# The opening of a decoder trunk: where the first shift vector is summed, and how the first matmul units follow

## The chip, the cores and the metric

The kernel runs on one core of one Trainium2 chip. Its time is the device time of one launch in microseconds (us). Three runs of the kernel before took 1204.4, 1201.04 and 1201.66 us, a median of 1201.66 us. The engines are named as in the profile: PE (matmuls; PEld its weight loads), DVE (vector), ACT (scalar), POOL (GpSimd) and SP, which here only issues transfers.

## The reference

Two layers act on a sequence of 256 rows of width 1024. Each layer is a SwiGLU feed-forward part (FFN), a token-mixing part and a second FFN, and each of the three reads a normalised and modulated input. Only the very first one matters here:

```python
c_act = jax.nn.silu(c)
mod = c_act @ w_ada[l] + b_ada[l]                      # 9 vectors of 1024
sh1, sc1, gt1, sh2, sc2, gt2, sh3, sc3, gt3 = jnp.split(mod, 9, axis=-1)
h = rmsnorm(x, ln_ffn1_g[l]) * (1 + sc1) + sh1         # modulate
x = x + 0.5 * gt1 * (silu(h @ w_gate) * (h @ w_up)) @ w_down
```

Each of the nine vectors is the product of one row of 1024 values with a 1024 x 1024 matrix: 4 MB of weights for one vector. The first FFN needs the scale vector `sc1` and the shift vector `sh1` before anything else.

## The kernel before, in words

Everything is held transposed, channels on partitions: `xT` is 8 blocks of 128 channels x 256 rows. A weight is brought in by granules of 1 MB (`raw`, four buffers, issued by SP) and cut into units of 128 output columns x 1024. The numbers are f32; a unit is split into a high part `hi` (a cast on ACT to the matmul format) and a low part `lo` (a subtraction, on DVE, for a few early units on POOL). There are six unit buffers. A product is three matmuls for each block: hi x hi, hi x lo, lo x hi, so a unit is 24 matmuls of 128x256.

A modulation vector is four granules of `w_ada`. DVE sums them: for each of eight blocks one instruction `acc = raw * c + acc` on 128x1024 (tiles `Lb` and `adaacc`, function `ada_step`). `extract` then sums over partitions with eight PE transposes and two reductions, and `complete` adds the bias.

The list `seq` sets the order in which granules are loaded and used (`plan_ffn`, `adaunit`). Before, it begins with the scale vector (0, 1), then the first gate granule, the first up granule, the second gate granule, then the four granules of the shift vector (0, 0), then the second up granule. SP issues a granule only when its buffer is released.

The first FFN starts without the shift (`first`, the branch where `G["sh"]` is None). Since the norm factor is one number for each row, `(x*gs) @ W` can be computed before the norm is known, and the shift's part `sh @ W` is added as a bias for each column. Six units (gate 0 and 1, up 0 and 1, gate 2 and 3) run one behind the other (`low_last`), then PE waits for the shift vector. With it, 96 narrow matmuls make `sh @ W` for the six units (tile `sh_b`, two stationary columns), and `turn_row` turns these rows into biases. Up 2 and 3, and everything behind, use the finished modulated input `H`.

Later phases do it in another way (the other branch of `first`): the input has two more columns that hold the split shift, so that a matmul of 258 columns gives `sh @ W` along with the rest, and the bias is copied from column 256 (`cols`). Four units start that way, and the fifth already uses `H`.

`columns(0, 1)` turns rows of small constants into columns: two PE transposes into the same PSUM tile `px`, each followed by a DVE copy (`colA`, `colB`). The second transpose may not start before the first copy has read `px`. `keep_warm` is a few matmuls whose result nobody reads.

The order on each engine is that of the program text; `pump` and `step_stream` put conversions and sums into it by modelled times. `down 0` below is the first unit of the first FFN's down projection, `pa<-Y,hi` in the profile: from there on PE does the same work in both kernels.

Of the kernel before, what the change touches and what calls it, by code (L numbers as in the profile page):

```python
# [177 lines left out]
def trunk(ctx, tc, t, out):  # L178
# [121 lines left out]
    def plan_ffn(l, which, ada):  # L300
        wg, wu, wd = (t[f"ffn{which}_w_{n}"][l] for n in ("gate", "up", "down"))
        jobs = []
        gd = {}
        key = ("f", l, which)

        def down(f):
            if f % 2 == 0:
                gd[f // 2] = rgran(wd, 128 * f)
            wunit(key + ("d", f), gd[f // 2], rview(f % 2))

        slots = FB - 2 if len(ada) > 4 else FB // 2
        start = 4 if key == ("f", 0, 1) else 0
        at = {}
        for i, item in enumerate(ada):
            at.setdefault(start + i * (slots - start) // len(ada), []).append(item)

        def extra(slot):
            for item in at.pop(slot, ()):
                adaunit(*item)

        for q in range(FB // 2):
            for n, w in (("g", wg), ("u", wu)):
                g = kgran(w, 256 * q, 256)
                for j in range(2):
                    wunit(key + (n, 2 * q + j), g, kview(256, j))
                if key == ("f", 0, 1) and (q, n) == (1, "g"):
                    for i in range(4):
                        adaunit(0, 0, i)
            if q:
                extra(2 * q - 2)  # L330
                for j in range(2):
                    down(2 * q - 2 + j)
                extra(2 * q - 1)
        down(FB - 2)
        down(FB - 1)
        assert not at
# [72 lines left out]
    for i in range(4):  # L409
        adaunit(0, 1, i)  # L410
# [68 lines left out]

    def ada_step(item):  # L480
        _, (l, v), g, i, _ = item
        raw = grans[g]["tile"].rearrange("p (k n) -> p k n", n=D)
        if i == 0:
            tag = "adaacc" if (l, v) in ADA["m", 0] + ADA["m", 1] or cfg["tag"] == "Lb" else "Lb"
            cfg["tag"] = tag
            while any(job[1].tensor.name.startswith(tag) for job in ada_wait):
                extract()
            ada_acc[l, v] = sb([128, D], tag)
        acc = ada_acc[l, v]
        for j in range(2):  # L490
            k = 2 * i + j
            c = c_act[:, k:k + 1]
            if k == 0:
                dve.tensor_scalar(acc, raw[:, j], c, 0.0, op0=OP.mult, op1=OP.add)
            else:
                dve.scalar_tensor_tensor(acc, raw[:, j], c, acc, op0=OP.mult, op1=OP.add)
        release(g)
        if i == 3:
            ada_wait.append([(l, v), acc, 0])
# [169 lines left out]
    def begin(gs, sh):  # L669
# [4 lines left out]
        if sh is not None:  # L674
            hi, lo = split_col(sh)
            for src, piece, k, n in ((hi, 0, 0, 6), (hi, 1, 6, 2), (lo, 2, 0, 3), (lo, 3, 3, 3), (lo, 4, 6, 2)):
                dve.tensor_copy(pieces[piece][:, :, S:S1], src[:, k:k + n].unsqueeze(2).to_broadcast([128, n, S1 - S]))
        return dict(gs=gs, sh=sh, parts=[(a[:, :S1 if sh is not None else S], b[:, :S1 if sh is not None else S])
                                         for a, b in zip(his, los)])
# [95 lines left out]


    scr_g = nc.dram_tensor("scr_g", [D], F32, kind="Internal").ap()

    def ffn(l, which, G, normed, gate_v, nxt):
# [4 lines left out]
        def act_fn(f, o):  # L784
            if bias and f < 4:
                s = normed_out(o[:, 0])
                act.activation(s, s, AF.Silu, bias=bias[2 + f])
            else:
                s = sb([128, S], "tmp2", bufs=4)
                act.activation(s, o[:, 0], AF.Silu)  # L790
# [107 lines left out]
        def first():  # L898
            keys = [key + (n, i) for n in "gu" for i in range(2)]
            if G["sh"] is not None:  # L900
                cols = [sb([128, 2], f"bias{i}") for i in range(2)]
                outs = [bank((128, S1)) for _ in range(2)] + [ps([128, S1], f"a{i}") for i in range(2)]
                norm = {}
                first_units(keys, outs, G, lambda: norm.update(h=normed([pump] * 3)))
                for i in range(2):
                    for j in range(2):
                        dve.tensor_copy(cols[i][:, j:j + 1], outs[2 * j + i][:, S:S + 1])
            else:
                keys += [key + ("g", i) for i in (2, 3)]
                pair = [ps([128, 2, S], f"a{i}") for i in range(2)]  # L910
                raws.extend(bank() for _ in range(2))
                outs = [pair[i][:, j] for j in range(2) for i in range(2)] + [o[:, 0] for o in raws]
                for kk, o in zip(keys, outs):
                    low_last(o, need(kk), G["parts"])
                for k in range(KB):
                    act.activation(nscr["t"][:, k], xT[:, k], AF.Copy, scale=G["gs"][:, k:k + 1])
                    gp.tensor_tensor(nscr["t"][:, k], nscr["t"][:, k], nscr["r"], op=OP.mult)
                while (0, 0) not in ada_acc or not ada_wait:
                    step_stream()
                both = sb([128, KB, 2], "sh_b", F32R)  # L920
                p = [ps([2, n, 128], tag) for n, tag in ((4, "a2"), (2, "m0"))]
                job = ada_wait[0]
                columns(0, 1)
                keep_warm(3)
                for h in range(2):
                    extract()
                    c = slice(4 * h, 4 * h + 4)
                    act.copy(both[:, c, 0], job[3][:, c])
                    dve.tensor_tensor(both[:, c, 1], job[3][:, c], both[:, c, 0], op=OP.subtract)
                for h in range(2):  # L930
                    for i, kk in enumerate(keys):
                        for k in range(4 * h, 4 * h + 4):
                            for x, w in enumerate(conv[kk]):
                                mm(p[i // 4][:, i % 4], both[:, k], w[:, k], k == 0 and x == 0 and i % 4 == 0, (k, x) == (KB - 1, 1))
                row = sb([2, 6, 128], "Wc")
                early = {}

                def rows_out():
                    act.copy(row[:, 0:4], p[0])
                    act.copy(row[:, 4:6], p[1])  # L940

                norm = dict(h=normed([lambda: None] * 3 + [lambda: [done(kk, 1, True) for kk in keys[:2]]], True))
                rows_out()
                early.update((i, normed_out(outs[i])) for i in range(4))
                act.preload_act_table_set("silu_and_others")
                for i, kk in enumerate(keys[2:]):
                    done(kk, 2 * (i == 3), True)

                def turn_row():
                    p = ps([128, 6, 2], "a3")  # L950
                    for i in range(6):
                        pe.transpose(p[:, i], row[:, i], ident[0:2, 0:2])
                    b = sb([128, 6], "bias0")
                    dve.tensor_reduce(b, p, axis=AX.X, op=OP.add)
                    bias.extend(b[:, i:i + 1] for i in range(6))
                    acc.extend(ps([128, 2, S], f"a{i}") for i in range(4))
                    for i in range(2):
                        first_act(i, early[i], early[2 + i], bias[i], bias[2 + i])

            if G["sh"] is not None:  # L960
                su = [normed_out(o) for o in outs]
                acc.extend(ps([128, 2, S], f"a{i}") for i in range(4))
                for kk in keys:
                    done(kk)
                act.preload_act_table_set("silu_and_others")
                for i in range(2):
                    first_act(i, su[i], su[2 + i], cols[i][:, 0:1], cols[i][:, 1:2])
                return norm["h"], None
            return norm["h"], turn_row

        bias, raws = [], []
        hparts, pending = first()
# [3 lines left out]
        for q in range(1, FB // 2):  # L976
            o = raws if raws and q == 1 else [bank() for _ in range(2)]
            blocks = [(j, i, key + (n, 2 * q + i)) for j, n in enumerate("gu") for i in range(2) if j or o is not raws]
            for j, i, kk in blocks:
                w = need(kk)  # L980
                if o is raws:
                    low_last(o[i][:, j], w, zip(*([x[:, k] for k in range(KB)] for x in hparts)), pending)
                    pending = None
                else:
                    for k in range(KB):
                        mm3(o[i][:, j], w, hparts, lambda a: a[:, k], lambda a: a[:, k], k == 0, k == KB - 1)
# [937 lines left out]
    cfg["lo_first"] = ["gp", "dve", "gp", "dve", "gp", "gp", "dve", "gp", "dve", "gp"]  # L1924
    columns(0, 0)
    step_stream()
    gs = need_mod(0, 1)
    G = begin(gs, None)
    keep_warm(3)
# [3 lines left out]
    step_stream()  # L1933
    rstd(sums)
# [56 lines left out]
```

## Time and profile before

| what | us |
|---|---|
| median of three runs (1201.04 to 1204.4) | 1201.66 |
| the profiled execution, its own time | 1202.57 |
| span of that execution's trace | 1200.8 |
| PE busy in the span | 1130.7 |
| DVE busy | 874.4 |
| ACT busy | 612.6 |
| POOL busy | 169.3 |

In the timeline a row gives the start, the duration and the engine, then the operation with the tile written, the tiles read and the shape; `xN` counts merged instructions, and brackets hold the idle time of the engine ahead of it and what ended that. An f32 matmul appears as two records. Buffer numbers are left out, so `pa` is any of the four accumulators and `pm` any of three working banks. [...]

### The profile page before, as it was taken

How to read it: one execution, taken by the hardware profiler on the slowest of the kernel's cores; microseconds unless marked ns; L12 is line 12 of the kernel's file. 1: busy time of each engine (PE TensorE's matmuls, PEld its weight loads, DVE VectorE, ACT ScalarE, POOL GpSimd, SP SyncE). 2: the span in 40 equal slices, each digit the busy share in tenths (PEclk: the TensorE clock that was granted, in tenths of full speed). 3: DMA queues.
4: the chain of work that ended last, by engine and by line, in shares of the span. 5: the costliest groups of instructions: out<-in, count | busy, mean ns of one | idle time of the engine just before them, and what ended most of it. 6: DMA issues, size and time to landing. Idle time of an engine off the chain costs nothing.

```text
span 1200.8 us, 22053 instructions
## 1 busy us (share of the span) xinstructions
PE 1130.7 (94%) x9085; PEld 1052.0 (88%) x9085; DVE 874.4 (73%) x1314; ACT 612.6 (51%) x1049; POOL 169.3 (14%) x213
## 2 busy tenths in 40 slices
PE   5799999999978789999999999999997899999997
PEld 4799999977767789999999999997876789999996
DVE  5778878757965788877778878774886759866554
ACT  4364443548367464434456544444654667544443
POOL 0610000011761010000000000001067401000001
PEclk9899999999999989999999999999999799999999
DMA  8759888836342558969865987892642334876640
GB/s 320 246 186 319 309 299 309 256 113 192 95 137 91 176 176 285 322 243 326 291 218 170 324 313 266 278 300 74 186 140 73 141 108 140 287 257 211 195 139 36
DMA packets 167661, 256.52 MB, mean 214 GB/s; under 512 B 8272, under 2 KB 134056, under 8 KB 167560
## 3 DMA queue, kind: packets, MB, share of 16 engines
q1 hardware_dynamic: 166536, 252.95, 62.6%
q0 software_dynamic: 1024, 2.16, 0.9%
q8 instruction: 71, 1.16, 0.4%
q14 instruction: 30, 0.25, 0.1%
HBM read 252.86 MB, written 2.23 MB: 212 GB/s over the span
## 4 chain that ended last, share of the span: by engine, by line
PE 71%; DVE 12%; ACT 6%; POOL 6%; issue 3%; DMA 1%; SPq 0%; POOLq 0%; DVEq 0%; ACTq 0%
PE pm L171 45%; PE pa L171 25%; DVE lo L171 3%; DVE adaacc L171 3%; PE px L171 2%; ACT hi L171 1%; POOL W L171 1%; POOL cacc L171 1%; POOL T L171 1%; POOL Lb L171 1%; DVE mod L171 1%; ACT L171 1%; DVE tmp L171 1%; DVE Lb L171 1%; DVE Y L171 1%
## 5 line engine op out<-in xcount | busy, mean ns | idle before, releaser
L171 PE MATMUL pm<-H,hi 128*128 128x256 f32 x2816 | 507.7, 283 | 2.8 <-issue 1.6
L171 DVE TENSOR_TENSOR lo<-raw,hi 128x1024 fp32r<-128x1024 f32 (+1 forms) x300 | 362.1, 1226 | 131.8 <-ACT hi L171 131.3
L171 PEld LDWEIGHTS pm<-H,hi 128*128 128x128 f32 x2816 | 431.9, 189 | 5.9 <-issue 2.2
L171 ACT CAST hi<-raw 128x1024 fp32r<-128x1024 f32 (+1 forms) x306 | 311.3, 1040 | 195.3 <-PE pm L171 80.7
L171 PE MATMUL pm<-H,lo 128*128 128x256 f32 x1408 | 392.4, 280 | 1.2 <-DVE lo L171 1.2
L171 PEld LDWEIGHTS pm<-H,lo 128*128 128x128 f32 x1408 | 264.5, 189 | 1.7 <-DVE lo L171 1.6
L171 PE MATMUL pa<-Y,hi 128*128 128x256 f32 x1312 | 241.3, 286 | 4.5 <-DVE xT L171 4.5
L171 PEld LDWEIGHTS pa<-Y,hi 128*128 128x128 f32 x1312 | 204.1, 192 | 6.7 <-DVE xT L171 5.3
L171 PE MATMUL pa<-Y,lo 128*128 128x256 f32 x656 | 185.8, 283 | 0.0
L171 PEld LDWEIGHTS pa<-Y,lo 128*128 128x128 f32 x656 | 127.3, 194 | 0.0
L171 POOL TENSOR_TENSOR xin_LT<-xin_LT 128x256 f32<-128x256 f32 x35 | 27.1, 775 | 664.8 <-ACT xin_LT L171 662.4
L171 ACT CAST Y<-tmp 128x256 fp32r<-128x256 f32 x88 | 35.8, 406 | 131.5 <-DVE tmp L171 131.5
L171 DVE SCALAR_TENSOR_TENSOR adaacc<-raw,c_act,adaacc 128x1024 f32<-128x1024 f32 x70 | 95.5, 1365 | 1.6
L171 DVE SCALAR_TENSOR_TENSOR Lb<-raw,c_act,Lb 128x1024 f32<-128x1024 f32 x56 | 71.8, 1283 | 4.2 <-DMA raw<-in_w_ada_dram 3.0
L171 POOL TENSOR_TENSOR cacc<-cacc,ctap 128x256 f32<-128x256 f32 x54 | 52.3, 973 | 122.0 <-DVE cacc L171 112.8
L171 DVE TENSOR_TENSOR Y<-tmp,Y 128x256 fp32r<-128x256 f32 x88 | 37.4, 425 | 41.5 <-ACT Y L171 41.5
L171 PE MATMUL pm<-Y,raw 128*128 128x256 f32 x288 | 66.8, 384 | 0.0
L171 PEld LDWEIGHTS pm<-Y,raw 128*128 128x128 f32 x288 | 53.4, 190 | 8.9 <-issue 1.0
L171 PE MATMUL pa<-hi,Y 128*128 128x512 f32 x176 | 54.8, 393 | 0.0
L171 ACT ACTIVATE tmp<-pm 128x256 f32<-128x256 f32 x84 | 31.8, 378 | 43.9 <-PE pm L171 43.7
L171 DVE TENSOR_REDUCE mod<-px 128x4 f32<-128x512 f32 x34 | 23.4, 689 | 34.3 <-PE px L171 34.2
L171 DVE SCALAR_TENSOR_TENSOR cacc<-hc,colB,cacc 128x256 f32<-128x256 f32 x66 | 36.0, 562 | 10.3 <-POOL cacc L171 9.4
(309 smaller groups left out, 1342.9 us busy)
## 6 DMA issues: line engine op xcount, KB each, us to landing
raw<-in_w_ada_dram SPq DMA_DIRECT2D x70, 1024.0 KB
raw<-in_ffn_w_gate_dram SPq DMA_DIRECT2D x44, 1024.0 KB
raw<-in_ffn_w_up_dram SPq DMA_DIRECT2D x44, 1024.0 KB
raw<-in_ffn_w_down_dram SPq DMA_DIRECT2D x44, 1024.0 KB
raw<-in_w_in_dram SPq DMA_DIRECT2D x12, 1024.0 KB
raw<-in_w_in_dram SPq DMA_DIRECT2D x20, 512.0 KB
raw<-in_w_out_dram SPq DMA_DIRECT2D x16, 512.0 KB
raw<-in_w_in_dram SPq DMA_DIRECT2D x4, 768.0 KB
```

The costliest lines, as they stand in the source:

```text
L171: return getattr(real, op)(*args, **kw)
```

## The change

The shift vector's four granules stand directly behind those of the scale vector in the list, ahead of all FFN weights. Their sum moves from DVE to PE: 16 matmuls with one stationary column (`c_act`) and 512 moving columns of `raw`, in f32, give the vector as a row in two PSUM banks (`ada_rows`); ACT and DVE copy the row out, eight small transposes turn it into a column, and the bias is added. The first FFN then starts as later phases do, with 258 columns, but unit by unit (`first_serial`) instead of all four block by block. The six-unit branch with `sh_b`, `turn_row` and the POOL product is gone, and so are both `keep_warm` calls. `columns(0, 1)` now stands behind the conversions that follow the first four units. The vectors for later parts are spread from slot 2 on instead of slot 4.

```diff
-        start = 4 if key == ("f", 0, 1) else 0
+        start = 2 if key == ("f", 0, 1) else 0
...
-                if key == ("f", 0, 1) and (q, n) == (1, "g"):
-                    for i in range(4):
-                        adaunit(0, 0, i)
...
-    for i in range(4):
-        adaunit(0, 1, i)
+    for v in (1, 0):
+        for i in range(4):
+            adaunit(0, v, i)
...
+    def ada_rows(raw, g, i):
+
+        if i == 0:
+            ada_acc[0, 0] = [ps([1, 512], f"a{2 + h}") for h in range(2)]
+        for k in (2 * i, 2 * i + 1):
+            for h in range(2):
+                mm(ada_acc[0, 0][h], c_act[:, k:k + 1], raw[:, k % 2, 512 * h:512 * h + 512], k == 0, k == KB - 1)
+        release(g)
+        if i < 3:
+            return
+        row = sb([1, D], "adaacc")
+        act.copy(row[:, 0:512], ada_acc[0, 0][0])
+        dve.tensor_copy(row[:, 512:], ada_acc[0, 0][1])
+        p = ps([128, KB], "x")
+        for k in range(KB):
+            pe.transpose(p[:, k:k + 1], row[:, 128 * k:128 * k + 128], ident[0:1, 0:1])
+        m = sb([128, KB], "mod0", bufs=2)
+        dve.tensor_copy(m, p)
+        complete(m, 0, 0, slice(0, KB))
+        mods[0, 0] = m
...
+    def first_serial(keys, outs, G, between):
+
+        for i, (key, o) in enumerate(zip(keys, outs)):
+            low_last(o, need(key), G["parts"], between if i == 0 else None)
...
+            opening = key == ("f", 0, 1)
+            (first_serial if opening else first_units)(keys, outs, G, lambda: norm.update(h=normed([pump] * 3, opening)))
...
+            for kk in keys:
+                done(kk)
+            if opening:
                 columns(0, 1)
-                keep_warm(3)
...
-    cfg["lo_first"] = ["gp", "dve", "gp", "dve", "gp", "gp", "dve", "gp", "dve", "gp"]
     columns(0, 0)
-    step_stream()
     gs = need_mod(0, 1)
     G = begin(gs, None)
-    keep_warm(3)
+    rstd(sums)
     for k in range(KB):
         scaled_hi(G, k)
         scaled_lo(G, k)
-    step_stream()
-    rstd(sums)
+    for k in range(KB):
+        dve.scalar_tensor_tensor(nscr["t"][:, k], xT[:, k], gs[:, k:k + 1], nscr["r"], op0=OP.mult, op1=OP.mult)
+    for i in range(4):
+        step_stream()
+    G["sh"] = need_mod(0, 0)
+    G["shift"](G["sh"])
+    cfg["lo_first"] = ["gp", "dve", "gp", "dve"]
```

On PE, from the scale vector's last transposes (`pa_190`) on, the kernel before has three `keep_warm` matmuls, and the first unit follows at once:

```order
L171 MATMUL pa_190<-kc,Lb 128x128 [waits PE_49]
L171 MATMUL pa_190<-kc,Lb 128x128 x3
L171 MATMUL pa_203<-xin_LT,ones 128x256 [waits DVE_49]
L171 MATMUL pa_203<-xin_LT,ones 128x256 x2
L171 MATMUL pa_246<-S6a,hi 128x256 [waits Activation_49] x6
```

At the same place the changed kernel has the 16 sums (`pa_222` and `pa_223` in turn) and the eight small transposes, and only then the first unit (`pm_295`); its second sum waits for DVE to read `pa_183`:

```order
L171 MATMUL pa_183<-kc,Lb 128x128 [waits PE_49]
L171 MATMUL pa_183<-kc,Lb 128x128 x3
L171 MATMUL pa_222<-raw,c_act 1x512 [waits DMAHW4_49]
L171 MATMUL pa_223<-raw,c_act 1x512 [waits DVE_49]
...
L171 MATMUL px<-kc,adaacc 128x1 [waits Activation_49]
L171 MATMUL px<-kc,adaacc 128x1 x3
L171 MATMUL px<-kc,adaacc 128x1 [waits DVE_49]
L171 MATMUL px<-kc,adaacc 128x1 x3
L171 MATMUL pm_295<-S6a,hi 128x258 [waits DVE_49,Activation_49]
```

The sums stand ahead of the units, where before they ran on DVE beside them.

On DVE, the copy `colA` from `px` (rows 0 to 22 of it, read by PE's next transpose) stands before directly behind the shift vector's sum:

```order
L171 SCALAR_TENSOR_TENSOR adaacc<-raw,c_act,adaacc 128x1024 [waits DVE_49]
L171 SCALAR_TENSOR_TENSOR adaacc<-raw,c_act,adaacc 128x1024 [waits DMAHW1_49,DVE_49]
L171 SCALAR_TENSOR_TENSOR adaacc<-raw,c_act,adaacc 128x1024 [waits DMAHW2_49,DVE_49]
L171 COPY colA<-px 128x23 [waits PE_49]
L171 COPY colB<-px 128x98 [waits PE_49]
```

In the changed kernel the same copy stands behind the fourth unit's bias (`pa_298`), four products with the norm factor (`tmp`) and four weight conversions (`lo`):

```order
L171 COPY bias_294<-pa_298 128x1 [waits PE_49]
L171 TENSOR_TENSOR tmp_423<-pm_295,rstd 128x256
L171 TENSOR_TENSOR tmp_425<-pm_296,rstd 128x256
L171 TENSOR_TENSOR tmp_427<-pa_297,rstd 128x256
L171 TENSOR_TENSOR tmp_429<-pa_298,rstd 128x256
L171 TENSOR_TENSOR lo<-raw,hi 128x1024 [waits Activation_49]
L171 TENSOR_TENSOR lo<-raw,hi 128x1024 [waits DMAHW3_49,Activation_49]
L171 TENSOR_TENSOR lo<-raw,hi 128x1024 [waits Activation_49]
L171 TENSOR_TENSOR lo<-raw,hi 128x1024 [waits DMAHW4_49,Activation_49]
L171 COPY colA<-px 128x23 [waits PE_49]
L171 COPY colB<-px 128x98 [waits PE_49]
```

PE's second transpose, `px<-kc,rowsB`, waits for `colA` in both kernels, and in the changed one the fifth unit, the first that uses `H`, stands behind it.

## Rows read from the trace of the kernel before

**Rows 1.** The page, busy time of each engine over the span.

```profile
PE 1130.7 (94%) x9085; PEld 1052.0 (88%) x9085; DVE 874.4 (73%) x1314; ACT 612.6 (51%) x1049; POOL 169.3 (14%) x213
```

**Rows 2.** Timeline of PE, from the first unit to behind down 0.

```profile
25.89 1.11 PE L171 MATMUL pa<-S6a,hi 128*128 128x256 f32 x6
...
43.89 0.23 PE L171 MATMUL px<-kc,rowsA 23*128 23x23 f32 x1
49.93 0.42 PE L171 MATMUL px<-kc,rowsB 98*128 98x98 f32 x1 [5.81 <-DVE colA L171]
...
55.23 0.22 PE L171 MATMUL pa<-hi,sh_b 128*2 128x128 f32 x1 [0.55 <-DVE sh_b L171]
...
60.99 1.98 PE L171 MATMUL pm<-H,hi 128*128 128x256 f32 x15
64.18 0.38 PE L171 MATMUL pm<-H,hi 128*128 128x256 f32 x1 [1.22 <-DVE H L171]
64.50 0.53 PE L171 MATMUL pa<-kc,Wc 2*128 2x2 f32 x6
...
70.35 0.40 PE L171 MATMUL pa<-Y,hi 128*128 128x256 f32 x2
...
76.00 0.40 PE L171 MATMUL pm<-H,hi 128*128 128x256 f32 x2
...
87.31 0.40 PE L171 MATMUL pa<-Y,hi 128*128 128x256 f32 x2
```

**Rows 3.** Waits of PE from 60 to 270 us: total, times, longest.

```profile
PE pa L171 <- DVE xT L171: 0.9, 1, 0.9
```

**Rows 4.** Stretches with the granted clock: PE, PEld, DVE, ACT, POOL, clock, DMA.

```profile
28.00:32.00 4.00, 4.00 (x36) 4.00 (x35) 2.38 (x3) 3.97 (x7) 1.87 (x1) 1.00 0.36 97
...
50.00:52.00 2.00, 2.00 (x6) 1.64 (x7) 0.26 (x1) 0.00 (x0) 1.05 (x2) 0.50 1.10 333
...
55.00:56.00 1.00, 0.77 (x13) 0.77 (x14) 0.92 (x3) 0.00 (x0) 0.00 (x0) 0.91 0.01 4
...
65.00:67.00 2.00, 2.00 (x12) 2.00 (x12) 1.67 (x4) 0.64 (x2) 1.59 (x1) 0.60 0.73 272
67.00:70.00 3.00, 3.00 (x21) 3.00 (x20) 2.29 (x3) 1.03 (x3) 1.82 (x1) 0.70 0.42 166
```

**Rows 5.** Timeline of DVE in the opening, and one row of a later opening.

```profile
23.94 0.68 DVE L171 TENSOR_REDUCE mod<-pa 128x4 f32<-128x512 f32 x1
...
36.47 13.32 DVE L171 SCALAR_TENSOR_TENSOR adaacc<-raw,c_act,adaacc 128x1024 f32<-128x1024 f32 x7
49.71 0.17 DVE L171 COPY colA<-px 128x23 f32<-128x23 f32 x1
...
53.86 0.69 DVE L171 TENSOR_REDUCE mod<-px 128x4 f32<-128x512 f32 x1 [3.21 <-PE px L171]
...
55.01 0.17 DVE L171 TENSOR_TENSOR sh_b<-mod,sh_b 128x4 fp32r<-128x4 f32 x1 [0.26 <-ACT sh_b L171]
...
64.05 1.41 DVE L171 TENSOR_TENSOR tmp<-pa,rstd 128x256 f32<-128x256 f32 x4
...
425.27 4.62 DVE L171 TENSOR_TENSOR lo<-raw,hi 128x1024 fp32r<-128x1024 f32 x4
```

**Rows 6.** Timeline of PE in the first mixing part: f32 matmuls of other shapes.

```profile
238.61 0.60 PE L171 MATMUL pm<-S6a,wab 128*12 128x257 f32 x2
239.14 1.13 PE L171 MATMUL pm<-S6a,raw 128*128 128x257 f32 x4
...
269.87 1.02 PE L171 MATMUL pa<-tmp,kc 128*128 128x512 f32 x2
270.73 0.59 PE L171 MATMUL pm<-Y,raw 128*128 128x256 f32 x2
```

**Rows 7.** Timeline of POOL: the first low part there.

```profile
21.24 2.34 POOL L171 TENSOR_TENSOR lo<-raw,hi 128x1024 fp32r<-128x1024 f32 x1 [20.78 <-ACT hi L171]
```

**Rows 8.** Groups of ACT over the span: busy us, mean ns, idle before.

```profile
L171 ACT CAST hi<-raw 128x1024 fp32r<-128x1024 f32 x298 | 304.9, 1045 | 195.3 <-PE pm L171 80.7 <-DMA raw<-in_ffn_w_gate_dram 60.7 <-PE pa L171 34.7
```

More of the change, by code (lines that the diff above doesn't have):

```diff
@@ L482, in ada_step @@
         raw = grans[g]["tile"].rearrange("p (k n) -> p k n", n=D)
+        if (l, v) == (0, 0):
+            return ada_rows(raw, g, i)
         if i == 0:
@@ L673, in begin, with shift @@
         los = [pieces[2][:, k] for k in range(3)] + [pieces[3][:, k] for k in range(3)] + [pieces[4][:, k] for k in range(2)]
-        if sh is not None:
+        def shift(sh):
             hi, lo = split_col(sh)
@@ L677, in begin @@
                 dve.tensor_copy(pieces[piece][:, :, S:S1], src[:, k:k + n].unsqueeze(2).to_broadcast([128, n, S1 - S]))
-        return dict(gs=gs, sh=sh, parts=[(a[:, :S1 if sh is not None else S], b[:, :S1 if sh is not None else S])
-                                         for a, b in zip(his, los)])
+        if sh is not None:
+            shift(sh)
+        return dict(gs=gs, sh=sh, parts=list(zip(his, los)), shift=shift)
     def begin_whole(gs, sh, w):
@@ L784, in act_fn @@
         def act_fn(f, o):
[L785 to L790, printed above, removed]
+            s = sb([128, S], "tmp2", bufs=4)
+            act.activation(s, o[:, 0], AF.Silu)
             dve.tensor_tensor(s, s, o[:, 1], op=OP.mult)
@@ L899, in first @@
             keys = [key + (n, i) for n in "gu" for i in range(2)]
[L900 to L918, printed above, removed]
-                    step_stream()
-                both = sb([128, KB, 2], "sh_b", F32R)
-                p = [ps([2, n, 128], tag) for n, tag in ((4, "a2"), (2, "m0"))]
-                job = ada_wait[0]
-                columns(0, 1)
-                keep_warm(3)
[L925 to L971, printed above, removed]
@@ L972, in ffn @@
-        hparts, pending = first()
+            cols = [sb([128, 2], f"bias{i}") for i in range(2)]
+            outs = [bank((128, S1)) for _ in range(2)] + [ps([128, S1], f"a{i}") for i in range(2)]
+            norm = {}
+            opening = key == ("f", 0, 1)
+            (first_serial if opening else first_units)(keys, outs, G, lambda: norm.update(h=normed([pump] * 3, opening)))
+            for i in range(2):
+                for j in range(2):
+                    dve.tensor_copy(cols[i][:, j:j + 1], outs[2 * j + i][:, S:S + 1])
@@ L973, in ffn @@
+            su = [normed_out(o) for o in outs]
+            acc.extend(ps([128, 2, S], f"a{i}") for i in range(4))
+            for kk in keys:
+                done(kk)
+            if opening:
+                columns(0, 1)
+            act.preload_act_table_set("silu_and_others")
+            for i in range(2):
+                first_act(i, su[i], su[2 + i], cols[i][:, 0:1], cols[i][:, 1:2])
+            return norm["h"]
+        hparts = first()
         last = list(range(FB - 2 if nxt else FB - 3, FB))
@@ L976, in ffn @@
         for q in range(1, FB // 2):
-            o = raws if raws and q == 1 else [bank() for _ in range(2)]
-            blocks = [(j, i, key + (n, 2 * q + i)) for j, n in enumerate("gu") for i in range(2) if j or o is not raws]
+            o = [bank() for _ in range(2)]
+            blocks = [(j, i, key + (n, 2 * q + i)) for j, n in enumerate("gu") for i in range(2)]
             for j, i, kk in blocks:
                 w = need(kk)
[L981 to L986, printed above, removed]
+                for k in range(KB):
+                    mm3(o[i][:, j], w, hparts, lambda a: a[:, k], lambda a: a[:, k], k == 0, k == KB - 1)
                 done(kk)
@@ L1932, in trunk @@
         scaled_lo(G, k)
-    step_stream()
-    rstd(sums)
+    for k in range(KB):
+        dve.scalar_tensor_tensor(nscr["t"][:, k], xT[:, k], gs[:, k:k + 1], nscr["r"], op0=OP.mult, op1=OP.mult)
[4 more added lines that the diff above has]
+    cfg["lo_first"] = ["gp", "dve", "gp", "dve"]
     for _ in range(4):
```

## The prediction, as it was made before the result was known

> **What bounds the kernel now.** I read the page's busy times first: PE works in 94% of the span, no other engine in more than 73% [rows 1]. Then the waits of PE: from 60 to 270 us it stands 1.22 us at 64, still in the opening [rows 2], and 0.9 us near the end of the first FFN [rows 3], no more. So from down 0 on, which PE starts at 70.35 us [rows 2], there is no slack in that FFN that could absorb a delay or that a gain could be lost in. The order of every engine behind the first FFN is the same in both kernels. The question is therefore one number: when does PE start down 0?
>
> The timeline of PE gives today's answer [rows 2]. Six units run from 25.89 to the transpose at 43.89. Then PE stands 5.81 us, put down to `colA`. DVE could not copy it earlier, since the sums of the shift vector ran until 49.7: seven of eight take 13.32 us, started at 36.47 [rows 5]. [...] From 55.23 to 60.99, 5.8 us, come the narrow `sh_b` matmuls. A second dip of the clock costs 1.6 us at half in 65 to 67 and 1.8 in 67 to 70, together 3.4 [rows 4]. Up 2 and up 3 fill the rest to 70.35.
>
> **The change, part by part, as a clock of marks.**
>
> *The sum on PE.* Sixteen matmuls, f32, one stationary column, 512 moving. The trace has no such shape; it has f32 with 512 moving columns and a full stationary: from 269.87 to 270.73, 0.86 us [rows 6]. Whether one column is cheaper is bounded by a narrow neighbour: 12 stationary columns with 257 moving take 0.53 us (238.61 to 239.14), and two with 128 stationary take 1.07, the next narrow one following at 240.21, which is 0.53 each [rows 6]. A narrow stationary gains nothing there, so I take 0.86; the lower bound is half of it (one record instead of two). The first sum can run when the last transposes are done, the second only when DVE has read `pa_183`: 23.94 + 0.68 = 24.62 [rows 5]. Fifteen more by 0.86 are 12.9, so the sums end at 37.5. Data are no limit: the granules take the places of three weight granules and of the shift's own first one, and in the kernel before those nine MB were in by about 29, since the rate from 28 to 32 is down to 97 GB/s [rows 4]; the last granule is wanted at about 34. The FFN weights now wait for these sums to release their buffers; the first gate granule is issued at about 27 and wanted at 39.
>
> *From the sum to the first unit.* DVE copies 512 values: 0.69, as the reduction of the same size [rows 5]. Four small transposes: 0.3, from six such between 64.50 and about 64.95 [rows 2], and 0.2 for the copy of the column. Adding the bias and the cast on ACT: from 53.86 to 55.01 less the 0.69 of the reduction, 0.46 [rows 5]. ACT then casts the first unit, 1.05 [rows 8], since that cast stands behind the shift's in ACT's queue; the five column copies on DVE run beside it. Sum 2.7: the first unit starts at 40.2. It starts at 25.89 today.
>
> *Four units of 258 columns.* Four units of 256 columns take 11.31 us (76.00 to 87.31 [rows 2]); two columns more add 1%, so 11.4. The first waits for its low part: POOL needs 2.34 [rows 7] from the cast's end, 42.5, and PE is there after two thirds of a unit, 42.1. That row had DVE idle beside it for most of its time; here DVE works, so I allow 0.4 to 1 and take 0.7. The fourth unit ends at 52.3.
>
> *A wait that the change builds.* PE's transpose of `rowsB` waits for `colA`, and that copy now stands on DVE behind the fourth unit's bias. Counting from 52.3: the bias copy 0.15, four products with the norm factor 1.41, four low parts 4.62, the copy itself 0.17 [rows 5]. All four low parts have their casts by then, so nothing shortens this. With 0.2 for the transpose, 6.55: the fifth unit starts at 58.9. PE has nothing else queued; the unit's own inputs, `H` and its weights, have long been ready. If I am wrong on the cover (low parts already done), it is 1.9; the order of DVE excludes that.
>
> *Four units with `H`.* 11.31 us at full clock [rows 2] would end at 70.2. But PE has stood 6.5 us, about as long as at 43.9, where the clock fell. The price is between 1.7 (3.4 us at half, as in the dip at 65) and 2.6 (5.25 us at half, as after the stop of the same kind) [rows 4]. I take 2.6, the row nearest in kind. Down 0 starts at 72.8.
>
> *What else goes.* The DVE sums (13.32 us and the first), the POOL product, `sh_b` and `turn_row` all go, but each of them only mattered through the mark at 70.35, which is accounted for. The vectors for later parts start two slots earlier; DVE is busy 73% over the span [rows 1] and PE waits for none of these sums in the rows behind 60 us, so nothing.
>
> **The sum.** 72.8 - 70.35 = 2.45 us later. The profiled execution took 1202.57 us, which would become 1205.0. It lies 0.9 above the median of the runs shown, inside their spread; on the median, 1201.66 + 2.45 = 1204.1. I predict 1204.1. With the low prices (half clock 1.7, POOL 0.4, and 0.2 less for the chain to the first unit) it is +1.0. A measurement of this kernel tells some 0.3%, 3.6 us, from no change, so this counts as the same, on the slow side: the change takes one stop away and builds another, and the 14 us by which the units start later just about use up `sh_b` and the sums on DVE.
>
> **The rivals.**
>
> *The clock falls at the first gap too.* Between 37.5 and 40.2 PE has only eight tiny transposes. In the kernel before, the clock fell at about 65.4 although PE had stood only 1.22 us shortly before, with small transposes behind it [rows 2, 4]. If the same happens here, 3.4 us at half fall into the four units: 1.7 more, +4.1, 1205.8, slower by just over 0.3%. Against it: the sums right before keep PE full, and at 65 the narrow matmuls had preceded. [...] Chance 0.25.
>
> *One-column sums do not hold the clock.* If PE's clock falls during the sums, from about 28 on, the eleven that are left take 1.72 each instead of 0.86: 9.5 us more, the first unit at 49.7, and the total at +12, 1213.6, clearly slower. For it: nothing in the trace has one stationary column. [...] It decides from the point at which the clock falls before some 33 us. Chance 0.10.
>
> *One-column sums are cheap.* At half of 0.86 the sums end at 31.1, behind the last data by two microseconds. Everything moves 6.4 earlier: -4.0, 1197.7, faster by 0.33%. For it: only the missing shape; against it: the 12-column rows. Other ways to a gain (casts or low parts shorter than priced) give at most 1.5 us. Chance 0.10 for all of that.
>
> *The second stop does not come.* If the four low parts were over when the fourth unit ends, the fifth unit would start 4.6 earlier and the clock would perhaps not fall: -4.7, 1197. But DVE works in order, and the low parts stand behind the bias copies, so this has no chance of its own beside the 0.10.
>
> **How the numbers follow.** The forecast, +1.0 to +3.6, has 0.55; slower by over 3.6 us takes the two clock rivals, 0.35; faster by over 3.6 takes 0.10. The range for 8 in 10: below, the low prices give 1202.7 and the runs spread by 0.6 under the median, and a part of the gains reaches to 1199.5; above, the first clock rival gives 1205.8, and with POOL and the chain to the first unit at their high ends 1207; a part of the second clock rival (a fall late in the sums) reaches to 1211. Left out are the full second rival and the cheap sums, some 0.17 together. The likeliest case's own range is 1202.7 to 1205.3.
>
> **What would show it right or wrong.** In the changed kernel's timeline of PE: sums of 0.86 us each from 24.6 to 37.5; the first `pm<-S6a` at about 40.2; a stop of some 6.5 us behind the fourth unit, put down to `colA`; a granted clock of 0.50 behind it for 3.4 to 5.3 us; down 0 at about 72.8. Sums at 0.43 or 1.72, or no stop at `colA`, would break the forecast at that step; so would any wait of PE over 1 us between down 0 and 225 us, which would mean that DVE or the transfers no longer keep up.

## The result, and the profile after

The changed kernel takes 1209.63 us (median of 5 runs, 1207.71 to 1212.17) against 1201.66: ratio 1.0063, interval 1.0041 to 1.0085. Forecast was 1204.1, so the likeliest case had the right sign, and its size, +2.45, was a third of the 8.0 measured. The profiled execution is the slowest of the five, 1212.17 with a span of 1210.4; against the profile before, the span grows by 9.6.

The page's busy row of PE, beside [rows 1], shows 82 fewer matmul records and yet 13 us more busy time. Fewer records are not less work: the sums are 32 long records, 30 of which take 13.04 us in the timeline below. The mean granted clock is lower too, 0.970 against 0.976.

```profile
PE 1143.5 (94%) x9003; PEld 1055.1 (87%) x9003; DVE 863.6 (71%) x1322; ACT 609.8 (50%) x1039; POOL 145.9 (12%) x201
```

The timeline of PE in the opening, which answers to [rows 2] (start, duration, then the idle time ahead and what ended it):

```profile
24.86 13.04 PE L171 MATMUL pa<-raw,c_act 128*1 128x512 f32 x30 [0.39 <-DVE mod L171]
37.83 0.41 PE L171 MATMUL px<-kc,adaacc 1*128 1x1 f32 x4
38.67 0.41 PE L171 MATMUL px<-kc,adaacc 1*128 1x1 f32 x4 [0.44 <-DVE adaacc L171]
40.71 0.98 PE L171 MATMUL pm<-S6a,hi 128*128 128x258 f32 x6 [1.63 <-ACT hi L171]
...
45.08 1.00 PE L171 MATMUL pm<-S6a,hi 128*128 128x258 f32 x6
...
53.93 0.24 PE L171 MATMUL px<-kc,rowsA 23*128 23x23 f32 x1
60.20 0.42 PE L171 MATMUL px<-kc,rowsB 98*128 98x98 f32 x1 [6.03 <-DVE colA L171]
60.33 0.78 PE L171 MATMUL pm<-H,hi 128*128 128x256 f32 x2
...
74.18 0.41 PE L171 MATMUL pa<-Y,hi 128*128 128x256 f32 x2
```

Down 0 starts 3.83 us later than at 70.35. The sums are what was priced: 30 records, two to a matmul, in 12.97 us, 0.86 a matmul. The stop at `colA` is there, 6.03 us. DVE shows why, as [rows 5] had it in pieces:

```profile
54.04 0.16 DVE L171 COPY bias<-pa 128x1 f32<-128x1 f32 x1 [1.97 <-PE pa L171]
54.11 0.75 DVE L171 TENSOR_TENSOR tmp<-pm,rstd 128x256 f32<-128x256 f32 x2
54.77 0.75 DVE L171 TENSOR_TENSOR tmp<-pa,rstd 128x256 f32<-128x256 f32 x2
55.44 4.62 DVE L171 TENSOR_TENSOR lo<-raw,hi 128x1024 fp32r<-128x1024 f32 x4
59.98 0.17 DVE L171 COPY colA<-px 128x23 f32<-128x23 f32 x1
```

The stretches of the opening, beside [rows 4]. A row has the stretch and its length, the busy time and instruction count of PE, PEld, DVE, ACT and POOL, then PE's granted clock as a share of its full speed, the DMA share and GB/s. The clock is 0.50 in the first unit (from 41.92 us on, for 3.41) and again in the first `H` units, the units that use `H` (from 58.98 on, for 6.83).

```profile
42.00:44.00 2.00, 2.00 (x11) 2.00 (x10) 2.00 (x1) 2.00 (x4) 2.00 (x2) 0.50 0.28 88
44.00:46.00 2.00, 2.00 (x13) 2.00 (x13) 2.00 (x2) 2.00 (x5) 2.00 (x1) 0.67 0.21 29
...
60.00:62.00 2.00, 1.80 (x9) 1.80 (x10) 1.01 (x5) 0.65 (x2) 0.00 (x0) 0.50 1.09 389
62.00:64.00 2.00, 2.00 (x11) 2.00 (x11) 1.10 (x3) 1.45 (x3) 0.00 (x0) 0.50 0.91 363
64.00:66.00 2.00, 2.00 (x12) 2.00 (x12) 1.23 (x1) 0.40 (x2) 0.00 (x0) 0.55 0.03 8
```

That explains 3.8 of the 9.6 us. To find the rest I compared the start of the same instruction in both timelines, at later and later places. From down 0 on both kernels have the same 8727 matmul records. Their order differs only between some 104 and 232 us, where the transposes of the vectors for later parts stand elsewhere (slot 2 instead of 4).

| PE's first instruction of | before | after | later by |
|---|---|---|---|
| down 0 | 70.35 | 74.18 | 3.83 |
| the dense 32x32 matmuls, first mixing part | 362.62 | 365.34 | 2.72 |
| the transposes that end that part | 405.22 | 413.88 | 8.66 |
| the dense 32x32 matmuls, second mixing part | 944.95 | 955.37 | 10.42 |

So 5.94 us are lost between 365 and 414, in instructions that stand in the same order in both kernels. What stands there is a dense run, 168 matmuls of 32x32 one behind the other. The timeline of PE, first of the kernel before, then of the changed one:

```profile
362.62 0.92 PE L171 MATMUL pa<-Lb,Wc 32*32 32x32 f32 x69 [1.50 <-ACT E L171]
363.36 0.21 PE L171 MATMUL pa<-Wc,Lb 32*32 32x32 f32 x1
363.37 0.20 PE L171 MATMUL pa<-Lb,Wc 32*32 32x32 f32 x3
363.40 1.01 PE L171 MATMUL pa<-Wc,Lb 32*32 32x32 f32 x95
```

```profile
365.34 0.92 PE L171 MATMUL pa<-Lb,Wc 32*32 32x32 f32 x69 [1.52 <-ACT E L171]
366.08 0.21 PE L171 MATMUL pa<-Wc,Lb 32*32 32x32 f32 x1
366.09 0.20 PE L171 MATMUL pa<-Lb,Wc 32*32 32x32 f32 x3
366.12 0.76 PE L171 MATMUL pa<-Wc,Lb 32*32 32x32 f32 x66
371.39 0.64 PE L171 MATMUL pa<-Wc,Lb 32*32 32x32 f32 x29 [4.51 <-issue]
```

In the changed kernel the run is cut after 139 of its 168 matmuls; PE stands 4.51 us and waits for nothing that the profile shows ("issue"). From 369.6 us, inside the stop, the clock is halved for 13.6 us. One stretch of the kernel before, at 1.00, and three of the changed kernel:

```profile
370.00:375.00 5.00, 3.85 (x23) 3.00 (x24) 4.29 (x12) 3.55 (x11) 0.00 (x0) 1.00 0.00 0
```

```profile
370.00:375.00 5.00, 3.61 (x40) 2.85 (x39) 3.81 (x9) 2.06 (x6) 0.00 (x0) 0.50 0.02 3
375.00:380.00 5.00, 5.00 (x64) 3.93 (x64) 2.01 (x6) 0.88 (x3) 0.00 (x0) 0.50 0.00 0
380.00:385.00 5.00, 5.00 (x91) 4.27 (x90) 1.83 (x4) 3.58 (x11) 0.00 (x0) 0.68 0.01 3
```

The kernel before has one shorter stop of this kind, behind the dense run of its second mixing part:

```profile
949.40 0.77 PE L171 MATMUL pm<-H,hi 128*128 128x256 f32 x2 [1.57 <-issue]
```

My supposition was that PE had no instructions to run. The page of the kernel before counts 71 packets, 1.16 MB, on the queue `q8 instruction`, 16,384 bytes each. Shared out over its 9085 matmuls and as many weight loads, that is 256 instructions a packet, 64 bytes each: an estimate that takes the queue to be PE's. In the transfers of the changed kernel from 367 to 371.5 us one such packet comes behind the last of 4.19 MB that had run since 355 (it starts at 369.2):

```profile
q1 hardware_dynamic: 81, 0.27, 15.5%
q8 instruction: 1, 0.02, 1.4%
```

**Theory A (supply).** It supposes that a packet is called for at fixed places of PE's instruction stream, and that PE runs dry if it gets a fixed number of instructions further before the packet is in; no view shows a call. I counted PE's records (matmuls, weight loads and its semaphore instructions) up to the start of each packet. The earliest packets start some 155 past a multiple of 256: of the 71 of the kernel before, 68 start 153 to 241 past one, and three 10 to 51 past the next. I take some 155 as the call, an estimate from these counts. In the changed kernel the dense run begins 15 instructions behind a call so placed, in the kernel before 177; the change removed 162 instructions ahead of it. **Rival B:** the stop belongs to the time at which transfers run, which the change moved as well. An instruction's place, below, is its number in this count.

### The profile page after: what moved, and what is told of

It is laid out like the page before. It is cut to its first block, busy times and chain, and to the rows that moved or that the text cites. A ratio compares the mean times of both kernels' runs of the same rounds, so it can differ in the third digit from the quotient of the medians.

```text
span 1210.4 us, 21887 instructions
## 1 busy us (share of the span) xinstructions
PE 1143.5 (94%) x9003; PEld 1055.1 (87%) x9003; DVE 863.6 (71%) x1322; ACT 609.8 (50%) x1039; POOL 145.9 (12%) x201
## 4 chain that ended last, share of the span: by engine, by line
PE 77%; DVE 11%; POOL 5%; ACT 3%; issue 2%; DMA 1%; SPq 0%; POOLq 0%; ACTq 0%; DVEq 0%
PE pm L171 47%; PE pa L171 28%; DVE lo L171 3%; PE px L171 2%; DVE adaacc L171 2%; POOL W L171 1%; ACT hi L171 1%; POOL T L171 1%; POOL Lb L171 1%; POOL cacc L171 1%; DVE tmp L171 1%; DVE mod L171 1%; DVE Y L171 1%; DVE Lb L171 1%; DMA xin_LT<-in_x_dram 1%
## 5 line engine op out<-in xcount | busy, mean ns | idle before, releaser
L171 PE MATMUL pm<-H,hi 128*128 128x256 f32 x2848 | 517.5, 283 | 0.0
L171 DVE TENSOR_TENSOR lo<-raw,hi 128x1024 fp32r<-128x1024 f32 (+1 forms) x304 | 369.7, 1233 | 146.6 <-ACT hi L171 146.4
L171 PEld LDWEIGHTS pm<-H,hi 128*128 128x128 f32 x2848 | 440.3, 190 | 2.7 <-issue 0.3
L171 PE MATMUL pm<-H,lo 128*128 128x256 f32 x1424 | 400.0, 281 | 1.5 <-DVE lo L171 1.5
L171 PEld LDWEIGHTS pm<-H,lo 128*128 128x128 f32 x1424 | 270.1, 190 | 1.9 <-DVE lo L171 1.9
L171 PE MATMUL pa<-Y,hi 128*128 128x256 f32 x1312 | 243.8, 287 | 4.0 <-DVE xT L171 4.0
L171 DVE SCALAR_TENSOR_TENSOR adaacc<-raw,c_act,adaacc 128x1024 f32<-128x1024 f32 x63 | 82.4, 1308 | 1.4
```

The costliest lines, as they stand in the source:

```text
L171: return getattr(real, op)(*args, **kw)
```

## The experiments

Ratios are to the kernel before, measured again beside each group: 1201.67 us (24 runs) for 1, 2, 7 and 8, 1201.66 (23) for 3, 4, 9 and 10, 1201.89 (17) for 5, 6 and 11. A padding matmul, one whose result nobody reads, has two records and two weight loads: four places.

**1 and 2. Padding at PE's first wait, in the changed kernel and in the kernel before** (20 and 24 times, behind the load of `c_act`).

```
+    for _ in range(20):
+        nc.tensor.matmul(p[:, 127:128], ident, ident[:, 0:1], start=True, stop=True, ...)
```

> After with 20 one-column matmuls (128x128 of the identity, one column of it, written to a bank that nobody reads) on PE behind the first transpose, in the 6 us in which PE waits for x anyway. Nothing else is moved: they only push every later PE instruction 80 places (20 x 2 matmul records and 2 x 20 weight loads) down its stream. Theory A (instruction supply): PE's instructions come in packets of 16,384 B, 71 of them for 9085 matmuls and 9085 weight loads (256 instructions a packet); in after one packet lands too late in the dense run of 32x32 matmuls at 366 us because the run begins just behind the place at which the next packet is called for. 80 places further on the run no longer crosses it: the stop of 4.51 us (waits on 'issue') is gone or under 0.5 us, the clock stays at 1.00 behind it, the lag behind the kernel before no longer grows by 6 us between 362 and 434 us; time 1203 to 1205 us, ratio to before 1.001 to 1.003. Rival B (the stop comes from when the transfers run, or from anything else the change shifts in time): the stop stays, ratio 1.006 +- 0.002. Down 0 is at 74.2 by both.

> The kernel before with 24 such one-column matmuls at the same place (96 places). Theory A: they put the dense 32x32 run of the first mixing part at the same place in a 256-instruction packet as in after; the kernel before, with none of the change in it, gets a stop of 3 to 5 us on 'issue' there and a fall of the clock behind it, and loses its own stop of 1.57 us in the second mixing part: net +3 to +6 us, ratio 1.0025 to 1.005. Rival B: 1.000 +- 0.001, no stop in the first mixing part. Down 0 stays at 70.4 by both.

Measured: 1206.65 us, ratio 1.0044 (1.0028 to 1.0061), and 1208.38, 1.0057 (1.0041 to 1.0072). The stop went in the first and came in the second, 3.06 us after 138 matmuls. But my padding was not free: a record took 0.217 us, 8.70 in all, and down 0 moved by 2.1 (76.32) and 3.3 (73.65). From down 0 to the end of the first mixing part, which leaves that out, the changed kernel takes 339.7 us and with padding 333.9; the kernel before 334.9 and with padding 338.6. The stops went as A says; the times needed a cleaner pair.

**3 and 4. The same places without the time:** 32x32 stationary, one column.

```
-        nc.tensor.matmul(p[:, 127:128], ident, ident[:, 0:1], ...)
+        nc.tensor.matmul(p[0:32, 127:128], ident[0:32, 0:32], ident[0:32, 0:1], ...)
```

> After with 20 matmuls of 32x32 by one column at the start, in place of the 20 of 128x128 whose 40 records took 0.217 us each and held the opening up by 2.8 us. The same 80 places on PE, but no time: the x transposes start at 9.2 as in after. Theory A (instruction supply): no stop on 'issue' at the 32x32 run; from down 0 to the next part's first transposes 334 us as in the run with 128x128 padding (333.9) instead of 339.7; down 0 at 74.2; time 1209.6 - 5.8 = 1203.8, ratio 1.001 to 1.003, which is what the prediction's own sum came to (+2.45). Rival: the stop's going in that run was owed to the shift of 2 us in time, not to the places: then it is back here, ratio 1.006.

> The kernel before with 24 matmuls of 32x32 by one column at the start (96 places), with no time lost at the opening. Theory A: stop of 3 to 4.5 us on 'issue' at the 32x32 run of the first mixing part, half clock behind it for 1.3 us; its own stop of 1.57 us in the second mixing part gone; down 0 at 70.4; net +2.5 to +4.5 us, ratio 1.002 to 1.004, by nothing but the count of instructions ahead. Rival: 1.000 +- 0.001.

Measured: 1203.43 us, ratio 1.0011 (0.9996 to 1.0026), and 1203.28, 1.0013 (1.0002 to 1.0023). The padding took 2.3 and 2.7 us of a wait of 6, down 0 stands at 74.32 and 70.24. Nothing but the count of instructions ahead takes the changed kernel's 1.0063 to 1.0011 and gives the kernel before a stop that it did not have. The run of the padded changed kernel, whole again, and of the padded kernel before, cut:

```profile
365.72 0.92 PE L171 MATMUL pa<-Lb,Wc 32*32 32x32 f32 x69 [1.61 <-ACT E L171]
366.46 0.21 PE L171 MATMUL pa<-Wc,Lb 32*32 32x32 f32 x1
366.47 0.20 PE L171 MATMUL pa<-Lb,Wc 32*32 32x32 f32 x3
366.50 1.01 PE L171 MATMUL pa<-Wc,Lb 32*32 32x32 f32 x95
```

```profile
362.28 0.76 PE L171 MATMUL pa<-Wc,Lb 32*32 32x32 f32 x65
366.07 0.64 PE L171 MATMUL pa<-Wc,Lb 32*32 32x32 f32 x30 [3.03 <-issue]
```

The second fell short of the +2.5 expected (+1.6). The kernel before loses its own stop of 1.57 in the second mixing part, and from that run to the end it needs 253.2 us in this profile instead of 255.8. Not all of that is the stop's: the profiles of runs 2 and 5, without it too, need 255.2 and 255.1, and there the clock is at half for 13.7 us behind the run, where here it stays at 1.00.

**5 and 6. Places that free the kernel before of its stop too, and places that must give two.** 44 of the small matmuls in the kernel before, 56 in the changed one.

> The kernel before with 44 small matmuls at the start, 176 places, which puts both dense 32x32 runs where the padded after has them: neither crosses a packet's late edge. Theory A: its own stop of 1.57 us in the second mixing part and the half clock behind it go, nothing comes in the first; ratio 0.997 to 0.999. So the change itself, both kernels free of such stops, costs 1203.4 - 1199.5 = 3 to 5 us, what the opening's marks show (3.8). Rival: 1.000.

> After with 56 small matmuls at the start, 224 places. Theory A by places alone: the run of the second mixing part (46 places behind the call for the next packet in after) now stands 14 behind it, as the first did (15) when it stopped: a stop of 3 to 4.5 us on 'issue' appears there, where no kernel so far had one inside the run, after some 135 to 140 of its 168 matmuls. The first mixing part's run calls for its packet 17 places into itself: a stop at some 155 of its 168 matmuls or just behind it. Rival: the stop belongs to the first mixing part alone: none in the second.

Measured: 1200.18 us, ratio 0.9985 (0.9975 to 0.9995), no row on "issue". With 56, one run, 1211.39 us: 3.31 us after 155 matmuls in the first mixing part, and in the second, where no run had been cut before:

```profile
953.61 0.78 PE L171 MATMUL pa<-Wc,Lb 32*32 32x32 f32 x67
957.32 0.64 PE L171 MATMUL pa<-Wc,Lb 32*32 32x32 f32 x28 [2.93 <-issue]
```

B falls: with the opening's times all but kept (runs 3 and 4), the stop goes where the count puts it. Adding the place of the run behind the call and the instructions done in it until PE stops gives 15 + 278, 17 + 276 (both padded kernels before), -17 + 310 and 14 + 280 (56 small ones): 293 or 294 each time. The stop of the kernel before in its second mixing part fits as well: its run calls 49 instructions into itself, and PE stands behind 342, run and three more matmuls, 342 - 49 = 293. These sums hang on where I put the call; the next two readings do not. All seven stops of the record (run 8 has one more) stand at the same place, 193 past a multiple of 256. And each time PE goes on 2.2 to 2.4 us after a packet has started, in the stop or just ahead of it (in the changed kernel 369.2 and 371.39).

**7. Filling the first gap.** Four matmuls of 256 f32 columns between the small transposes and the first unit; 16 of the slow padding matmuls keep the 80 places.

```
+        q = psum.tile([128, S], F32, name="pa3", tag="pa3", bufs=1)
+        for _ in range(4):
+            nc.tensor.matmul(q, ones, nscr["sq"][:, 0], start=True, stop=True, ...)
```

> After with 16 of the one-column matmuls at the start and 4 matmuls of 256 f32 columns (0.43 us each) into a bank that is read no more, between the eight small transposes of the shift and the first unit: PE is busy in 39.1 to 40.8 instead of idle for 1.63 us; same 80 places in all as the kernel with 20, so the two differ by the filling alone. If the fall of the clock in the first unit comes from this gap: granted clock 1.00 in 42 to 46, first unit 1.6 us shorter, down 0 at about 72.6 instead of 74.2, time 1.6 us less than that kernel. If the clock falls for the small transposes as much as for the gap, or if DVE's lo at 47.5 ends the wait anyway: down 0 within 0.4 of 74.2 and no difference in time.

Measured: 1203.79 us, ratio 1.0022 (1.0009 to 1.0035), down 0 at 71.67 (76.32 with 20 slow ones). Of the 4.65 between them 1.8 is the shorter padding and 0.9 the sums of squares, whose 16 records took 5.41 us instead of 6.31. The clock stays at 1.00 from 40 to 48,

```profile
42.00:44.00 2.00, 1.71 (x14) 1.51 (x13) 2.00 (x2) 2.00 (x5) 2.00 (x2) 1.00 0.06 19
```

and the first unit takes 3.55 us (40.34 to 43.89) instead of 4.50: 0.95, not 1.6, as POOL's low part is then what is late (PE waits 0.29 for it). So the fall came with the gap, and it cost 0.95; the other 1.0 came in the `H` units.

**8. The row constants ahead of the first unit.**

```
     G["shift"](G["sh"])
+    columns(0, 1)
...
-            if opening:
-                columns(0, 1)
```

> After with the two transposes and copies of the row constants (columns(0, 1)) done behind the shift's split, ahead of the first unit, instead of behind the four units. No padding, so the stop at 366 us stays by theory A. My theory of the opening: the wait of 6.03 us on colA goes, but the next thing late is the first lo of the second pair of units, done by DVE at 55.44 + 1.16 = 56.6; so the H units start at 56.7 instead of 60.3 (-3.7). Down 0 at 70.5 if the clock still falls in a gap of 2.7 us, 67.9 if it holds. Time -3.7 to -6.3 of 1209.6: 1203.3 to 1206, ratio 1.0013 to 1.0036. Rival: colA's wait was all of it, the H units follow at 54.2 and down 0 is at 65.6: 1201, ratio 0.9995. Rival: the two transposes in the chain to the first unit delay it by as much as they save later: ratio 1.006.

Measured: 1200.72 us, ratio 0.9990 (0.9978 to 1.0002), down 0 at 63.90. My own theory failed, the first rival held: no wait is left behind the fourth unit, as the timeline shows,

```profile
52.35 0.41 PE L171 MATMUL pa<-Q,lo 128*128 128x258 f32 x2
52.59 0.40 PE L171 MATMUL pm<-H,hi 128*128 128x256 f32 x2
```

because the next two units had been converted early; the four low parts that DVE does there are of later units. 10.3 us at down 0: 6.4 for the stop with the transposes, 2.5 for the half clock behind it, and 1.3 by which the shift's sums began earlier (23.59 against 24.86), since the sums of squares ahead took 5.41 us in this execution and 6.75 in the other. The medians moved by 8.9. At the 32x32 run it still stops, 3.10 us, 14 + 280 places behind the call.

**9 and 10. Both cures, and the gap filled by two matmuls on top.**

> After with columns(0, 1) ahead of the first unit (down 0 came at 63.9 with that alone, ratio 0.999) and the 20 small matmuls: its remaining stop of 3.10 us at the 32x32 run and the half clock behind it (about 1.3) go too. Down 0 at 63.9, no 'issue' row; 1200.7 - 4.4 = 1196.3 us, ratio 0.995 to 0.9965. If the two gains aren't separate (the gain at down 0 is eaten by a wait further back): above 0.998.

> The last one with 2 matmuls of 256 f32 columns (0.86 us) between the shift's small transposes and the rows' transposes, and 18 small ones at the start, 80 places in all. In after with columns early the clock still fell at 40.8 to 44.2. If the filling is enough, the clock is 1.00 from 22 on through the units: first unit 0.8 to 1.6 us shorter, 1195 us, ratio 0.994 to 0.9955. If the gap that is left (0.5 us and the small transposes) is enough for a fall: no difference to the last, 1196.3.

Measured: 1195.63 us, ratio 0.9942 (0.9928 to 0.9956), and 1196.10, 0.9946 (0.9931 to 0.9962). The first beats both kernels; the gains add up, 5.1 us for the 20 matmuls where 4.4 was expected. But only the stop went, not the half clock behind it: behind the uncut run the clock falls too, to half for 10.2 us.

```profile
358.00:368.00 10.00, 10.00 (x84) 7.80 (x85) 8.29 (x21) 5.64 (x19) 0.94 (x1) 0.50 0.01 2
```

The filling is worth nothing more that can be measured. It did keep the clock at 1.00 through all units, and the first unit took 3.55 us instead of 4.50; but in its profiled execution the shift's sums had begun 1.04 later (24.65 against 23.61), again behind slower sums of squares (6.44 us against 5.41), so down 0 came out the same, 64.02 against 63.94.

**11. The shift summed on DVE again**, load order and serial units as changed, 36 small matmuls to keep the places.

```
-        if (l, v) == (0, 0):
-            return ada_rows(raw, g, i)
```

> After, but the shift vector summed as before: 8 multiply-adds on DVE (TENSOR_SCALAR and SCALAR_TENSOR_TENSOR, about 1.36 us each by [rows 5]) and eight 128x128 transposes, in place of 16 matmuls on PE; the load order and the four units one behind the other stay as in after. 36 small matmuls at the start keep the count of PE instructions as in the padded after (64 fewer go ahead), so compare with that (1203.4). My theory: DVE is free for it at 31.5, ends at 42.4, the vector is there some 4.5 us later than from PE, and PE, idle from 23 to 43, has a fallen clock for the first unit: down 0 at 79 to 82 instead of 74.3, time 1208 to 1211, ratio 1.005 to 1.008. Rival: the matmul sums win nothing, since something else (the weights' lo at 46) holds the first unit anyway: down 0 within 1 of 74.3, ratio 1.001.

Measured: 1211.11 us, ratio 1.0073 (1.0058 to 1.0087), down 0 at 80.08. Down 0 came as expected: the sums on PE are worth 5.8 us there (74.32 with them). PE waits for DVE, and its clock is at half from 27.5 to 51.4:

```profile
41.22 1.09 PE L171 MATMUL px<-kc,adaacc 128*128 128x128 f32 x4 [18.07 <-DVE adaacc L171]
```

## Why the prediction was right and wrong

| step | forecast | measured |
|---|---|---|
| sums end | 37.5 | 37.83 |
| first unit | 40.2 | 40.71 |
| four units | 12.1 us | 13.22 us |
| stop with its transposes | 6.55 us | 6.40 us |
| four `H` units | 13.9 us | 13.85 us |
| down 0 | 72.8 | 74.18 |
| from down 0 to the end | no change | +5.8 us in the profile |

*Where it landed.* The measured 1209.63 lies in the range for 8 in 10, 1199.5 to 1211, but above the likeliest case's own, 1202.7 to 1205.3, and this was luck. The room above was left for a fall of the clock late in the sums, and through the sums the clock was 1.00. What filled it the prediction did not have: a stop of PE at 367 us, 4.51 us on "issue", which I put down to late instructions.

*What held.* The one-column f32 sum costs as much as the row with a full stationary [rows 6], 0.86 us; the chain to the first unit is 0.2 longer than its sum; the stop that the change builds has its size and its cause, and its price in half clock was the larger of the two taken [rows 4]: 13.85 us for the four `H` units against 11.31 at full clock, 2.5 where 2.6 was taken. The 5.25 us of half clock behind that term stand in the trace of the kernel before: the clock is 0.50 from 48.35 to 55.18 us, and PE works again from 49.93. In the changed kernel it is 0.50 until 65.81, 5.6 us of it behind PE's restart at 60.20. Both rivals on the sums fell: the clock is 1.00 all through them, and 0.86 is not 0.43.

*What was mis-sized.* "The clock falls at the first gap too" had a chance of 0.25, an estimate of mine, and a price of 1.7; it came true and cost 0.95 us (run 7). The trace of before had shown such a fall behind small transposes [rows 4], and the row of 42 to 44 us, 0.50, shows it here.

*What failed.* The step from down 0 to the end of the kernel: "each of them only mattered through the mark at 70.35", and the order behind the first FFN is the same, so nothing was added there. The order is the same, but the change removed 162 instructions ahead, and so the dense run of the first mixing part took another place in the count: PE stopped in it for 4.51 us and went on 2.2 us after a packet of instructions had started. That this packet was late is theory A; what the runs show is that the stops went and came with the count.

By the medians, the change with neither kernel stopped costs 1203.43 - 1200.18 = 3.2 us (1 to 5, an estimate from the intervals of the two ratios), near the forecast of 2.45. The padding that takes the changed kernel's stop away gains 1209.63 - 1203.43 = 6.2, the one that takes the kernel before's own away 1201.89 - 1200.18 = 1.7. That 3.2 + 6.2 - 1.7 comes near the 8.0 measured is no proof, since such differences must add up; the profile bears the middle one out, with 5.94 us lost between 365 and 414, 4.51 of them the stop. In the profiles of the two kernels without a stop (runs 3 and 5) the lag is 2.8 us at down 0, 2.1 at the first dense run, 4.8 at the second and 3.6 at the end, so behind down 0 the two are not quite alike even then. The row to see the stops was there: PE's waits over the whole span of the kernel before have this row, and I had cut them off at 270 us [rows 3].

```profile
PE pm L171 <- issue: 1.6, 1, 1.6
```

*Left open.* Between 74 and 365 us the lag shrinks by 1.1 us, and between 414 and 955 it grows by 1.8; I did not follow either. What part of the cost is the half clock behind a dense run is not shown: in the first mixing part it falls in all five executions with a stop (10.2 to 13.7 us at half), but also in three of the eight without (6.8 to 10.2). Why a packet would start over 3 us behind the place that I take for its call is not shown: weights were in transfer ahead of the stops (until 369 us in the changed kernel, until 947 in the kernel before), but no run took them away. The places of calls and stops are counts of trace records, of which a few may be missing.

## What to carry to other kernels

Read PE's waits on "issue" over the whole span before and after a change; where they differ behind the last changed instruction, count PE's instructions ahead of the densest run and shift it by a few idle ones, before judging the change by its total. A change of 0.3% was here hidden under 0.5% of such luck, of either sign. And of a copy that somebody waits for, ask first whether it can go ahead of what stands before it in its engine's queue: moving two transposes gave more here than the change cost.

## What I had not expected of the hardware

In the kernel before, 71 packets of 16,384 bytes were brought in on `q8 instruction` while it ran, the first at 30.1 us, the last at 1176.3. In the dense runs of 168 matmuls of 32x32, each about 11 ns, or just behind one, PE stood seven times over all executions for 1.57 to 4.51 us on "issue", and went on 2.2 to 2.4 us after such a packet had started. Each of the seven stops stood 293 or 294 instructions behind the call as I placed it, and at the same place, 193, in its 256. A one-column f32 matmul with 128x128 stationary took 0.217 us a record, with 32x32 stationary 0.057 in the same place: the first padding moved down 0 by 2.1 and 3.3 us, the second by 0.14 at most. And the 16 records of the sums of squares took 6.75 us in the changed kernel and 5.41 in run 8, by which alone the first unit came 1.3 us earlier: marks of two profiles are compared behind them.
